# An MLP block with fewer block products: x of two row pairs transposed by the DMA engines instead of TensorE, and cast a quarter sooner

## The chip, the cores and the metric

The kernel runs on one core of a Trainium2 chip. The metric is device time in microseconds (us) of one execution. Before the change three runs took 1533.64, 1534.25 and 1534.27 us, median 1534.25.

## What is computed

```python
x:  8 x 1024 x 1024 float32     # 8192 rows of 1024
w1: 1024 x 4096 float32
w2: 4096 x 1024 float32

h = x @ w1
h = 0.5 * h * (1 + np.tanh(np.sqrt(2 / np.pi) * (h + 0.044715 * h ** 3)))
return (h @ w2).astype(np.float32)
```

## The kernel before

**Tiles.** The rows of x are taken as 64 tiles of 128 rows, numbered c, and as 32 pairs of tiles, numbered k from 0 (so the fifth and sixth pair are k = 4 and 5, with the tiles 8 to 11). The columns of w1 are taken in four ranges, numbered r. Everything is multiplied in float16: each tile of x and each range of w1 is divided by its largest value first, and the scales are put back behind the products. So a tile of x goes through a chain: `load_x` (SP issues a DMA), `look_x` (ScalarE sums the absolute values of each row), `scale_x` (VectorE, two operations on one column), `cast_x` (VectorE makes the float16 tile x16), and a transpose into `xT[k]`, whose partitions are the contracted dimension. A range of w1 goes through a similar chain: `load_w1` (eight DMAs of 512 KB; those of range 0 are issued by SP, the others by GpSimd), `look_w1` (VectorE or ScalarE), `widest_w1` (VectorE, which writes `spread`), `scale_w1` (TensorE transposes `spread` into `rows`, line 162; VectorE reduces it to the scale and its inverse), `cast_w1` and, from range 1 on, `sum_w1`.

**First product.** The first six pairs against range 0 run as plain products (class `Plain`): 28 quarters, numbered p from 0, of eight matmuls each; the four quarters 24 to 27 are pair 0 against range 1. Quarters 16 to 19 are pair 4 (tile 8 in quarters 16 and 17, tile 9 in 18 and 19), and quarters 20 to 23 are pair 5 in the same way. A quarter's sum is read by ScalarE (`e`, the tanh form of gelu, line 442), scaled to float16 by GpSimd (`g`, line 177), and the two results of a half are stored to DRAM (`gd`, line 451) by one DMA of 256 KB that SP issues. From unit 7 on (class `Quad1`) a pair and a range are multiplied as two-by-two blocks with seven block products instead of eight; these need sums of blocks of x (`sum_x`) and of w1 (`sum_w1`).

**Second product.** The stored `gd` is read back transposed, by DMA transposes, and is multiplied with sums of blocks of w2 by a scheme of 26 block products for each pair (`second`). It starts near 798 us of the span.

**Order.** All five engines follow an order that is written out by hand (`manual_schedule`). `early(p, f, ...)` puts a step behind quarter p; `between` does the same inside the first four quarters, and `plan(u, slot, ...)` inside unit u. What each engine, and the queue of DMAs that SP issues, does next is fixed by that order: an instruction that waits holds up all behind it on its engine. Each of SP's DMAs also waits for the DMA that SP issued eight before it, since there are eight completion semaphores.

**Buffers.** The pool `k2` has eleven buffers, shared in turn by `e`, `g2` (the 256 KB that a store reads), `junk` (what `look_x` writes beside its sums) and x16. A buffer is written anew only when its last reader is done: if that reader was a DMA, the next writer waits for the DMA to land.

**The lines touched.** The loop over pairs 2 to 5 (lines 637 to 649) puts `look_x` behind quarter p - 1, and `scale_x` and `cast_x` behind quarter p. p is 4 + h, 6 + h, 9 + h, 12 + h for pair 2, 3, 4, 5 and half h. The transposes of all first six pairs are `turn_x_pe` (line 209): eight TensorE transposes of 128 x 128 into a PSUM tile `turned` (line 216), and a copy into `xT` by ScalarE (line 221) for half 0 or by VectorE (line 223) for half 1. Those of tiles 8 to 11 stand behind quarters 13, 15, 17 and 19. From pair 6 on the kernel uses `turn_x` (line 203): one DMA transpose of 256 KB that SP issues (line 207).

Of the kernel before, what the change touches and what calls it, by code (L numbers as in the profile page):

```python
# [79 lines left out]
def kernel(  # L80
# [7 lines left out]
    nc = tc.nc  # L88
# [58 lines left out]
    V, S, G = nc.vector, nc.scalar, nc.gpsimd  # L147
# [477 lines left out]
    def plan(u, slot, f, *args):  # L625
        assert 0 <= u, (f, args)
        todo.setdefault((u, slot), []).append((f, args))
# [6 lines left out]
    def early(p, f, *args):  # L634
        plan(p // 4, p % 4, f, *args)

    for k in range(2, FIRST):
        for h in range(2):
            c = 2 * k + h
            p = (4, 6, 9, 12)[k - 2] + h  # L640
            early(p - 1, look_x, c)
            early(p, scale_x, c)
            early(p, cast_x, c, V)
            if h:
                early(p, factors_of_block, k, 0, V)
                early(p, factors_of_block, k, 1, G)
            if k > 3:
                early((2, 5)[k - 4], load_x, c, wpool, "w")
            early(4 * k - 2 + 2 * h - (k > 2), turn_x_pe, c, V if h else S)
    for k in first:  # L650
        for i in range(4):
            if k == 1:
# [43 lines left out]
    for k in list(middle) + list(last):  # L696
        a = at[k] if k in middle else at[last[0]]
        for h in range(2):
            c = 2 * k + h
# [206 lines left out]
```

## Time and profile before

| | |
|---|---|
| median of three runs | 1534.25 us |
| the profiled execution | 1534.61 us |
| its span | 1532.8 us |
| mean granted TensorE clock | 1.0 of full speed |
| TensorE matmul busy | 1519.6 us (99%) |
| VectorE / ScalarE / GpSimd busy | 1183.0 / 734.5 / 479.6 us |
| DMA queue that SP issues on | 71.7% of 16 engines' span |
| DMA queue that GpSimd issues on | 2.6% |

The span is the time from the first to the last instruction in the trace; 1.8 us of the execution lie outside it. PE is TensorE's matmuls, PEld its weight loads, DVE is VectorE, ACT is ScalarE, POOL is GpSimd, SP is the engine that issues most DMAs. In a list of instructions the first two columns are start and duration in us, and a bracket holds the idle time of that engine just before, with what ended it. In a list of waits the numbers are the total in us, the number of waits and the longest. In a chain of work each row is start, duration and what was running.

### The profile page before, as it was taken

To read this page: it belongs to the slowest core of one execution; us is meant where nothing else is said; L and a number is where in the kernel's file an instruction comes from. 1 tells how busy PE (TensorE), PEld (TensorE's weight loads), DVE (VectorE), ACT (ScalarE), POOL (GpSimd) and SP (SyncE) were. 2 spreads that over 40 slices of the span, in tenths; PEclk is the share of its full clock that TensorE was granted. 3 is DMA by queue.
4 is the path that set the end of the run, shared out by engine and by line. 5 is a ranking of instruction groups with operands and counts; after the bars stand their busy time and mean duration, and the time that the engine had idled before them with its cause. 6 is when DMAs were issued, how large, how long until landed. Compare 5 with 4: busy or idle time off the path is not lost.

```text
span 1532.8 us, 28623 instructions
## 1 busy us (share of the span) xinstructions
PE 1519.6 (99%) x10398; PEld 1014.1 (66%) x10398; DVE 1183.0 (77%) x2409; ACT 734.5 (48%) x1302; POOL 479.6 (31%) x592
## 2 busy tenths in 40 slices
PE   7999999999999999999999999999999999999999
PEld 4444444444444444444448888888888888888888
DVE  6897787777777777574348888888888888888886
ACT  7778777777777777787762111111111111111111
POOL 5778554556666666554440000000000000000000
PEclk9999999999999999999999999999999999999999
DMA  9754989878789787784996777766866866866872
GB/s 349 241 185 128 293 276 301 250 227 238 215 247 263 222 270 222 240 215 128 273 285 143 140 134 141 143 137 135 154 133 128 160 133 122 165 133 130 152 142 80
DMA packets 459807, 293.94 MB, mean 192 GB/s; under 512 B 333840, under 2 KB 427024, under 8 KB 459664
## 3 DMA queue, kind: packets, MB, share of 16 engines
q1 hardware_dynamic: 456208, 279.52, 71.7%
q0 software_dynamic: 3456, 12.58, 2.6%
q8 instruction: 81, 1.33, 0.4%
q14 instruction: 62, 0.51, 0.1%
HBM read 96.99 MB, written 114.29 MB: 138 GB/s over the span
## 4 chain that ended last, share of the span: by engine, by line
PE 95%; DMA 1%; POOL 1%; ACT 1%; DVE 1%; issue 0%; ACTq 0%; POOLq 0%
PE pa L402 51%; PE pc L402 30%; PE pb L402 14%; DMA gd<-g 1%; POOL g L177 1%; DMA wn<-in_w_dram 0%; ACT e L442 0%; PE pb L414 0%; POOL wn L276 0%; DMA xn<-in_x_dram 0%; ACT junk L190 0%; PE turned L216 0%; POOL w L177 0%; DVE x L179 0%; ACT xT L221 0%
## 5 line engine op out<-in xcount | busy, mean ns | idle before, releaser
L402 PEld LDWEIGHTS <-gs 128*128 128x128 f16 x4608 | 450.8, 98 | 53.0 <-DVE gs L171 0.2
L177 POOL TENSOR_SCALAR g<-e,rs 128x512 f16<-128x512 f32 x446 | 363.8, 826 | 282.6 <-ACT e L454 250.2
L402 PEld LDWEIGHTS <-xs 128*128 128x128 f16 x1936 | 189.5, 98 | 227.7
L168 DVE TENSOR_TENSOR e<-pc,e 128x512 f32<-128x512 f32 x242 | 161.5, 685 | 200.6 <-ACT e L522 199.2
L402 PEld LDWEIGHTS <-xT 128*128 128x128 f16 x1676 | 163.1, 98 | 197.0 <-issue 1.6
L402 PE MATMUL pa<-w,gs 128*128 128x256 f16 x2304 | 288.3, 273 | 0.0
L402 PE MATMUL pa<-w,xT 128*128 128x512 f16 x1080 | 255.9, 379 | 1.2 <-DVE w L179 0.5
L454 ACT ACTIVATE e<-e,us 128x512 f32<-128x512 f32 x363 | 249.0, 719 | 2.4 <-DVE e L168 2.4
L402 PE MATMUL pc<-w,xs 128*128 128x512 f16 x968 | 248.4, 379 | 0.0
L402 PE MATMUL pa<-w,xs 128*128 128x512 f16 x968 | 248.4, 379 | 0.0
L402 PEld LDWEIGHTS <-gT 128*128 128x128 f16 x2048 | 200.4, 98 | 23.2
L575 ACT ACTIVATE o<-pa,vo 128x256 f32<-128x256 f32 x96 | 45.3, 472 | 332.3 <-PE pa L402 332.3
L402 PE MATMUL pc<-w,gs 128*128 128x256 f16 x1536 | 193.8, 273 | 0.0
L402 PE MATMUL pa<-w,gT 128*128 128x256 f16 x1024 | 132.7, 273 | 0.0
L402 PE MATMUL pb<-w,xT 128*128 128x512 f16 x484 | 124.2, 379 | 0.0
L571 DVE SCALAR_TENSOR_TENSOR o<-pc,vo,o 128x256 f32<-128x256 f32 x160 | 77.0, 481 | 57.6 <-PE pc L402 57.5
L513 ACT COPY e<-pa 128x512 f32<-128x512 f32 x121 | 70.9, 586 | 92.2 <-PE pa L402 85.8
L171 DVE TENSOR_TENSOR gs<-gT,gs 128x1024 f16<-128x1024 f16 x160 | 109.7, 686 | 1.6 <-DMA gT<-gd 1.6
L571 DVE SCALAR_TENSOR_TENSOR o<-pa,vo,o 128x256 f32<-128x256 f32 x192 | 91.9, 480 | 19.3 <-PE pa L402 19.3
L402 PE MATMUL pb<-w,gs 128*128 128x256 f16 x768 | 99.5, 273 | 0.0
L402 PE MATMUL pc<-w,gT 128*128 128x256 f16 x768 | 99.5, 273 | 0.0
L503 ACT COPY e<-pa 128x512 f32<-128x512 f32 x121 | 70.0, 579 | 49.2 <-PE pa L402 49.0
(104 smaller groups left out, 1447.8 us busy)
## 6 DMA issues: line engine op xcount, KB each, us to landing
gd<-g SPq DMA_DIRECT2D x484, 128.0 KB, 3.3
wn<-in_w_dram SPq DMA_DIRECT2D x72, 512.0 KB, 5.5
xn<-in_x_dram SPq DMA_DIRECT2D x64, 512.0 KB, 5.4
out_dram<-o SPq DMA_DIRECT2D x62, 512.0 KB, 3.6
w<-wd SPq DMA_DIRECT2D x25, 512.0 KB, 5.8
wn<-in_w_dram POOLq DMA_DIRECT2D x24, 512.0 KB, 6.0
wd<-wt SPq DMA_DIRECT2D x24, 512.0 KB, 5.0
gd<-g SPq DMA_DIRECT2D x14, 256.0 KB, 5.3
```

Of the source, the lines that this page charges most:

```text
L168: V.tensor_tensor(out=o, in0=a, in1=b, op=ALU.add)
L171: V.tensor_tensor(out=o, in0=a, in1=b, op=ALU.subtract)
L177: G.tensor_scalar(out=o, in0=i, scalar1=s, scalar2=1.0, op0=ALU.mult, op1=ALU.mult)
L402: nc.tensor.matmul(bank, lhsT=left(i), rhs=right[i], start=start and i == 0, stop=i == n - 1, skip_group_check=True,)
L454: S.activation(out=e, in_=src, func=ACT.Gelu_apprx_tanh, scale=self.u[half][s])
L503: S.copy(self.e11, self.pa)
L513: S.copy(self.e12, self.pa)
L571: V.scalar_tensor_tensor(out=o, in0=ps, scalar=v, in1=o, op0=ALU.mult, op1=ALU.add)
L575: S.activation(out=o, in_=ps, func=ACT.Copy, scale=v)
```

## The change

The casts of pairs 4 and 5 move one quarter forward, with the looks ahead of them: tile 8 from quarter 9 to 8, tile 9 from 10 to 9, tile 10 from 12 to 11, tile 11 from 13 to 12 (and their looks from 8, 9, 11, 12 to 7, 8, 10, 11). `factors_of_block` of the two pairs moves with them. The TensorE transposes of tiles 8 to 11, with their copies out of PSUM, are replaced by `turn_x` on SP's queue, which stands directly behind the cast.

```diff
     for k in range(2, FIRST):
         for h in range(2):
             c = 2 * k + h
-            p = (4, 6, 9, 12)[k - 2] + h
+            p = (4, 6, 8, 11)[k - 2] + h
             early(p - 1, look_x, c)
             early(p, scale_x, c)
             early(p, cast_x, c, V)
...
             if k > 3:
                 early((2, 5)[k - 4], load_x, c, wpool, "w")
-            early(4 * k - 2 + 2 * h - (k > 2), turn_x_pe, c, V if h else S)
+            if k > 3:
+                early(p, turn_x, c, nc.sync)
+            else:
+                early(4 * k - 2 + 2 * h - (k > 2), turn_x_pe, c, V if h else S)
```

At this place SP's queue held nothing but the stores of `gd`, one for each half of a pair. Now it holds three of them as before (pair 0, and the first half of pair 1), then the transposes of tiles 8 and 9, the store of pair 1's second half, the transpose of tile 10, the store of pair 2's first half, the transpose of tile 11, the store of pair 2's second half, and the rest as before.

## The prediction

> **What bounds the kernel now.** I read the page's shares first, then the chain that ended last, then TensorE's waits.
>
> ```profile
> PE 1519.6 (99%) x10398; PEld 1014.1 (66%) x10398; DVE 1183.0 (77%) x2409; ACT 734.5 (48%) x1302; POOL 479.6 (31%) x592
> ...
> PE 95%; DMA 1%; POOL 1%; ACT 1%; DVE 1%; issue 0%; ACTq 0%; POOLq 0%
> ```
>
> TensorE is busy for all but 13.2 us and carries 95% of the chain. So work taken from it shortens the run, unless it comes back as a wait. Its waits are few:
>
> ```profile
> PE turned L216 <- ACT x L175: 7.2, 1, 7.2
> PE rows L162 <- DVE spread L155: 1.0, 1, 1.0
> ```
>
> The first is the start. The second stands at 80 us, in unit 8, after the change; no wait is listed later, so whatever TensorE has gained by then stays to the end. The chain around 80 us shows what that wait hangs on:
>
> ```profile
> 69.37 6.13 DMA wn<-in_w_dram
> 75.53 1.22 DVE w1c L150
> ...
> 79.81 0.58 DVE spread L155
> ...
> 80.43 0.33 PE rows L162
> ```
>
> A load of w1's range 2, issued by GpSimd at 69.37, lands at 75.50; VectorE then works without a gap (look, sums, spread) until 80.39. And GpSimd's list shows why that load isn't issued sooner:
>
> ```profile
> 54.71 0.70 POOL L177 TENSOR_SCALAR g<-e,rs 128x512 f16<-128x512 f32 x1
> 56.56 0.70 POOL L177 TENSOR_SCALAR g<-e,rt 128x512 f16<-128x512 f32 x1 [1.15 <-ACT e L442]
> 57.23 1.55 POOL L177 TENSOR_SCALAR w<-wn,w1i 128x1024 f16<-128x1024 f32 x1
> ...
> 68.07 1.35 POOL L177 TENSOR_SCALAR g<-e,rs 128x512 f16<-128x512 f32 x2
> 69.37 1.48 POOL L276 DMA_DIRECT2D wn<-in_w_dram  x2
> ```
>
> GpSimd waits last at 56.56, for the gelu of quarter 19; from there to 69.37 it is packed, but for about 0.5 us.
>
> **What goes.** TensorE's list around one of the removed transposes:
>
> ```profile
> 41.98 1.89 PE L402 MATMUL pc<-w,xT 128*128 128x512 f16 x8
> 43.71 0.61 PE L216 MATMUL turned<-identity,x 128*128 128x128 f16 x8
> 44.16 1.89 PE L402 MATMUL pa<-w,xT 128*128 128x512 f16 x8
> ```
>
> From the transpose's start to the next quarter's is 0.45 us (44.16 - 43.71); the other three read the same (47.61, 51.51 and 55.52 to 48.06, 51.96 and 55.97). Four make **1.80 us**. Two copies of 1.00 us go from ScalarE and two of 0.69 from VectorE; none is waited for here, so they count nothing.
>
> **What of it is kept.** Three of the four transposes stand ahead of quarter 19, so its gelu frees GpSimd 3 x 0.45 = 1.35 us sooner. GpSimd being packed from there, the load at 69.37 and the spread at 80.39 come 1.35 sooner as well. TensorE comes 1.80 sooner: the wait of 0.97 grows by 0.45, and **1.35 us** are kept.
>
> **What is moved.** Looks and casts are as many and as long as before (look 1.06 + 0.19, cast 0.75 to 1.24 us). Following ScalarE's and VectorE's order with these rows, tile 8's cast ends near 37.4 (before 38.5), tile 9's near 39.8 (39.7: a look at w1 now stands between the two), tile 10's near 44.5 (44.3), tile 11's near 45.9 (46.9). Their rows were loaded long before: SP issued them by 19.7.
>
> **What is added.** Four transposes on SP's queue, the same shape as the 52 later ones. Those landed 3.0 to 9.3 us after issue, median 5.0. TensorE needs the tiles at quarters 16, 18, 20, 22, which without the transposes start at 47.2, 50.6, 54.2 and 57.6. At 9.3 the four land at 46.7, 49.1, 53.8 and 55.2, at 5.0 by 42.4 to 50.9. So TensorE doesn't wait for them; at the bound tiles 8 and 10 are within 0.5 us of doing so. Others do wait:
>
> - ScalarE. In the order and buffers of the changed kernel, the gelu of quarter 12 writes the buffer of tile 8's x16 and so waits for that transpose, quarter 13's waits for tile 9's, quarter 16's for tile 10's, and quarter 14's for the store of pair 1's second half, which SP issued near 34.4 and which now stands behind tile 9's transpose, near 41. Without these waits quarter 12 would be read at 42.2, quarter 13 at 43.9, quarter 14 at 45.6. At 5.0 us each the waits are 0.2, 1.0 and up to 1.5 us. TensorE has three banks of each kind, so it reaches the bank of quarter 12 only at quarter 18 (50.6); covered.
> - Behind quarter 15's gelu ScalarE has the last look at w1's range 1. It began at 48.55, the spread was done at 50.78, 2.23 later, and TensorE takes it at 53.68 (52.33 after the change). So the look must begin by 50.1.
> - The DMA engines. A transpose standing alone in the stretch 147.2 to 149.2:
>
> ```profile
> DMA packets 1076, 0.29 MB, mean 146 GB/s; under 512 B 1046, under 2 KB 1076, under 8 KB 1076
> ...
> q1 hardware_dynamic: 1076, 0.29, 72.6%
> ```
>
> 72.6% of 2.0 us is 1.45 us of all sixteen engines for 256 KB. In 36 to 48 us these are at 84 to 105%, with GpSimd's loads of range 1. Two transposes (2.9 us) get ahead of the last of them, two stores of about 0.7 us fall behind: it lands 1.5 us later than the 48.3 at which it landed (issued 42.16, 6.2 us), at 49.8, against 50.1. Cover 0.3 us; I charge 0.2.
>
> The Trainium skill (Advanced Engine Details and Errata, X-Bar Transpose) says that transposing DMAs are as fast as ordinary ones, 350 to 400 GB/s. The row is 181 GB/s, so the trace doesn't agree; by the rule the last load would land near 48.3, nothing would be charged, and the sum would be -1.35.
>
> **Sum.** -1.80 + 0.45 + 0.2 = -1.15 us: the profiled execution's 1534.61 becomes 1533.46. The median of the runs is 0.36 lower, 1534.25, and becomes **1533.1**.
>
> **Rivals.**
>
> *The wait takes it all (1534.3).* The transposes get only what GpSimd's loads leave. SP's queue, and idle engines, had some 2.6 to 2.9 us of DMA time from 38.7 to 48, and two transposes need 2.9. Tile 9 then lands near 48.5, the store behind it near 50, and ScalarE's order (look, gelu of 14, of 15, look) puts the spread at 53.4: TensorE stands 1.1 us at quarter 19, and GpSimd frees itself about when it did. For it: in this stretch stores of 256 KB were slow.
>
> ```profile
> gd<-g SPq DMA_DIRECT2D x6, 256.0 KB, 5.8
> ```
>
> Against: DMA bursts between the loads, in which a store is done at once; the quickest store took 2.4.
>
> *Slower (1535.7).* The two queues take turns by packets, not bytes. A store of 256 packets lost 3.4 us (5.8 - 2.4) beside the loads; a transpose has some 1024, so it would lose four times that, 13.6, or until GpSimd's loads are through at about 47.5. Tile 8 lands at 48.3, tile 9 at 49.8, the store at 51.2; the spread is done at 55.3; GpSimd's first pair of range 2 loads goes out at 56.3 instead of 53.19. Of these 3.1 us its idle 1.15 and 0.5 take up 1.65, so the end moves by +1.45. It decides from where tile 9 lands later than 47.3, and is a loss from about 48.5. With no idle used up it would be +3.1 (1537.4). Against it: in the stretches between two loads SP's queue got most of the engines. The Trainium skill (DMA: Bandwidth & Descriptors, Queues, rings and completion order) says that each DMA engine goes round the queues packet by packet, which, with the profile's packets, is this case; no transpose stands beside GpSimd's loads in this trace.
>
> *The wait at unit 8 goes (1531.5).* GpSimd's operations in the packed stretch vary between 0.7 and 1.84 us for the same tile; if they fall well, all 1.80 and the 0.97 are gained: -2.77.
>
> *It doesn't do what it says.* The tiles come too late for TensorE itself. At 14.5 us, half as long again as the longest of the 52, tile 9 lands at 54.3, 3.7 after quarter 18 should start: 1534.25 - 1.35 + 3.7 = 1536.6.
>
> **How the numbers follow.** The forecast 0.45, the wait that takes it all 0.25, slower by turns 0.20, unit 8's wait gone 0.05, TensorE waits 0.05. 0.2% of 1534.25 is 3.1 us, about what a measurement of this kernel can tell from no change: faster than 1531.2 needs more than all the gains above (0.03); slower than 1537.3 is the far end of the turns (0.06) and TensorE's waits (0.05); within, 0.86. Range 1531.8 to 1536.6: the forecast, no gain, and the slower case's own price.
>
> **What would show it.** Right: four groups on line 216 fewer; quarter 19 starting at 52.4; the load of range 2 issued near 68.0; `rows` at 79.1 with a wait near 1.4 us; no waits of TensorE for `xT` in quarters 16 to 23. Wrong: transposes that land later than 8 us; ScalarE's gelus of 12 to 14 waiting for DMAs past 47; a wait at quarter 19; `rows` of unit 8 at 80.4 or later.

## The result, and the profile after

The changed kernel takes 1538.44 us (median of 8 runs, 1537.41 to 1540.16), against 1533.78 for the kernel before (8 runs, 1533.08 to 1534.27): a ratio of 1.0033, 95% interval 1.0023 to 1.0042. It is slower by some 4.7 us. The profiled execution of after, one of the quickest of the eight, took 1537.74 us, 3.13 more than that of before, with a span of 1536.0 (+3.2).

The page's shares differ little: TensorE still carries the chain, with 10366 matmul instructions instead of 10398 (the 32 transposes are gone) and nearly the same busy time. TensorE's waits, as the list of waits has them after the change:

```profile
PE turned L216 <- ACT x L175: 7.2, 1, 7.2
PE rows L162 <- DVE spread L155: 4.1, 1, 4.1
```

It is the same line as before the change, but another place. TensorE's lists of before and then of after show where:

```profile
51.96 1.89 PE L402 MATMUL pa<-w,xT 128*128 128x512 f16 x8
53.68 0.27 PE L162 MATMUL rows<-identity,spread 128*128 128x128 f32 x1
```

```profile
50.68 1.89 PE L402 MATMUL pa<-w,xT 128*128 128x512 f16 x8
56.64 0.45 PE L162 MATMUL rows<-identity,spread 128*128 128x128 f32 x1 [4.07 <-DVE spread L155]
56.88 3.36 PE L402 MATMUL pc<-w,xT 128*128 128x512 f16 x8
60.07 1.89 PE L402 MATMUL pa<-w,xT 128*128 128x512 f16 x8
```

Three things are to be seen. Quarter 18 starts at 50.68 instead of 51.96: the gain of three turns is there. Then TensorE stands 4.07 us for range 1's `spread`, ahead of quarter 19, where it did not wait at all before. And quarter 19 itself takes 3.19 us up to the next one's start (60.07 - 56.88) instead of 1.73. Busy times in stretches of 1 us tell why; after the five engines' busy times come the granted clock, the DMA share and GB/s:

```profile
55.00:56.00 1.00, 0.00 (x0) 0.00 (x0) 0.00 (x0) 1.00 (x3) 0.81 (x2) 1.00 1.17 357
57.00:58.00 1.00, 1.00 (x4) 0.33 (x3) 0.93 (x5) 1.00 (x3) 1.00 (x2) 0.50 0.77 259
60.00:61.00 1.00, 1.00 (x7) 0.46 (x5) 1.00 (x1) 0.67 (x1) 0.70 (x1) 1.00 0.93 210
```

The granted clock is 0.50 behind the idle time, and 1.00 again from 60 on. So the differences between the two profiled executions, at the start of each step, are these: quarter 18 -1.28; `rows` 56.64 against 53.68, +2.96; quarter 20 +4.10 (0.13 more for a slower `rows`, 1.46 for the slow quarter 19, less the fourth turn of 0.45); unit 7 +4.11; unit 8 behind its `rows` +2.92, for the wait of 0.97 that stood there is gone; the end +3.2.

What the `spread` at 56.21 hung on, by the chain of waits of after:

```profile
41.76 0.25 SPq L207
42.10 11.49 DMA gd<-g
...
54.26 0.22 ACT e L442
...
54.83 1.15 ACT junk L286 x2
...
56.21 0.30 DVE spread L155
```

A store was held at SP behind the transpose of tile 9 until 42.10 and took 11.49 us; a gelu waited for its buffer, and behind this gelu ScalarE had its last look at range 1. ScalarE's waits in 25 to 72 us (total, number, longest) show two more of the kind:

```profile
ACT e L442 <- DMA xT<-x: 7.1, 2, 4.7
...
ACT e L442 <- DMA gd<-g: 1.3, 1, 1.3
```

And the DMA view of 38 to 50 us, of before and then of after (a line of an issue: count, KB each, median us from issue to landing):

```profile
DMA packets 1530, 3.32 MB, mean 276 GB/s; under 512 B 131, under 2 KB 922, under 8 KB 1528
...
q0 software_dynamic: 686, 2.48, 60.8%
...
wn<-in_w_dram POOLq DMA_DIRECT2D x3, 512.0 KB, 6.2
```

```profile
DMA packets 2695, 2.47 MB, mean 206 GB/s; under 512 B 2174, under 2 KB 2241, under 8 KB 2693
...
q0 software_dynamic: 514, 1.85, 70.5%
...
wn<-in_w_dram POOLq DMA_DIRECT2D x3, 512.0 KB, 9.8
...
xT<-x SPq DMA_TRANSPOSE x3, 10.5
```

More was asked of the DMA engines, and less was moved: 206 GB/s instead of 276. GpSimd's queue (q0) kept them busy longer for fewer bytes: 2.48 MB in 60.8% of 12 us is 340 GB/s of busy time, 1.85 MB in 70.5% is 219. The last load of range 1, issued at 42.69, landed 10.8 us later, at 53.5; before it landed at 48.3. The four transposes landed 6.5, 10.8, 10.5 and 5.7 us after issue.

### The profile page after: what moved, and what is told of

Its sections match the earlier page's. It is cut to its first block, busy times and chain, and to the rows that moved or that the text cites. A ratio compares the mean times of both kernels' runs of the same rounds, so it can differ in the third digit from the quotient of the medians.

```text
span 1536.0 us, 28563 instructions
## 1 busy us (share of the span) xinstructions
PE 1519.5 (99%) x10366; PEld 1012.8 (66%) x10366; DVE 1177.8 (77%) x2407; ACT 731.9 (48%) x1300; POOL 477.8 (31%) x592
## 3 DMA queue, kind: packets, MB, share of 16 engines
q8 instruction: 81, 1.33, 0.4%
## 4 chain that ended last, share of the span: by engine, by line
PE 97%; DMA 1%; DVE 1%; ACT 1%; issue 0%; SPq 0%; ACTq 0%; DVEq 0%
PE pa L402 52%; PE pc L402 31%; PE pb L402 14%; DMA gd<-g 1%; DVE x L179 0%; PE pb L414 0%; DMA xn<-in_x_dram 0%; DVE w1c L150 0%; PE turned L216 0%; ACT e L442 0%; ACT junk L190 0%; ACT w L175 0%; DVE xT L223 0%; ACT x L175 0%; ACT junk L286 0%
## 5 line engine op out<-in xcount | busy, mean ns | idle before, releaser
L503 ACT COPY e<-pa 128x512 f32<-128x512 f32 x121 | 69.9, 578 | 50.1 <-PE pa L402 50.0
```

The source lines that it names most:

```text
L503: S.copy(self.e11, self.pa)
```

## Experiments

The theory formed from these two traces: a DMA transpose and GpSimd's loads, side by side in two queues, slow each other down, so that loads, transposes and the store behind them land late, ScalarE's looks with them, and TensorE stands at quarter 19; its clock then adds to it. The rivals: the moved casts; more bytes in SP's queue; more packets, as in the prediction's slower rival; the buffers that ScalarE waits for. The first four kernels ran together, then the next four, then the last four; each ran beside the kernel before, whose medians were 1533.81, 1533.70 and 1533.67.

| kernel | median us | ratio to before, 95% | wait at quarter 19, us | wait at unit 8 | loads, transposes in 38 to 50, median us to landing |
|---|---|---|---|---|---|
| before | 1533.8 | | 0 | 0.97 | 6.2, none |
| after | 1538.44 | 1.0023 to 1.0042 | 4.07 | 0 | 9.8, 10.5 |
| 1 casts alone | 1533.75 | 0.9990 to 1.0007 | 0 | 0 | 6.1, none |
| 2 transposes alone | 1541.10 | 1.0026 to 1.0054 | 4.23, at quarter 18 | 0 | 8.0, 9.8 |
| 3 loads in SP's queue | 1534.57 | 0.9996 to 1.0013 | 0.66 | 0.99 | 5.9, 5.1 |
| 4 pair 5 alone, late | 1532.91 | 0.9985 to 1.0003 | 0 | 0.20 | 5.8, 3.6 |
| 5 padded wait | 1538.87 | 1.0024 to 1.0049 | 4.53 padding + 1.20 | 1.43 | 12.1, 10.5 |
| 6 plain copies | 1533.77 | 0.9992 to 1.0010 | 0 | 0.69 | 7.6, 6.9 |
| 7 copies in small pieces | 1532.56 | 0.9987 to 1.0005 | 0 | 0 | 6.2, 6.1 |
| 8 loads on SP, pair 5 late | 1533.52 | 0.9991 to 1.0009 | 0 | 1.24 | 6.6, 4.7 |
| 9 own buffers | 1537.75 | 1.0017 to 1.0034 | 3.24 | 0 | 10.3, 8.1 |
| 10 transposes on ScalarE's queue | 1539.29 | 1.0025 to 1.0050 | 3.56 | 0 | 9.4, 10.0 |
| 11 pair 4 as changed, pair 5 late | 1539.49 | 1.0022 to 1.0050 | 4.95 | 0 | 10.4, 7.9 |
| 12 as 8, range 2 on SP too | 1532.99 | 0.9983 to 1.0001 | 0 | 0 | 6.4, 4.8 |

### 1 and 2: the two halves of the change

Casts alone, against before; TensorE's transposes stay:

```diff
-            p = (4, 6, 9, 12)[k - 2] + h
+            p = (4, 6, 8, 11)[k - 2] + h
```

> Looks and casts of pairs 4 and 5 a quarter sooner, transposes left on TensorE. Theory A (the transposes on SP's queue and GpSimd's loads of range 1 hold each other up, so the scale of range 1 is late at quarter 19): the median stays within 0.6 us of before, 1533.2 to 1534.4, and TensorE doesn't wait at quarter 19. Theory B (the new order of looks and casts on ScalarE and VectorE makes the loss): 1537 to 1540, with the wait at quarter 19.

Transposes alone, against after; the casts stand where they stood:

```diff
-            p = (4, 6, 8, 11)[k - 2] + h
+            p = (4, 6, 9, 12)[k - 2] + h
```

> Transposes of tiles 8 to 11 by DMA, issued behind the casts where these stood before (quarters 9, 10, 12, 13). Theory A: slower than before by 3 to 6 us, like the change, with a wait of 3 to 6 us at quarter 19 and transposes that take 8 to 11 us to land beside GpSimd's loads. Theory B: no loss, 1532 to 1533.

The casts cost nothing: 1533.75, and TensorE has no wait at quarter 19. The transposes alone cost it all, 1541.1. In that trace the transposes stand later and landed 6.2 to 14.1 us after issue, and one was so late that TensorE waited for the tile itself, at quarter 18 (54.81):

```profile
PE pa L402 <- DMA xT<-x: 4.2, 1, 4.2
```

### 3 and 4: the transposes without a second queue beside them

Range 1's loads issued by SP, so that they share the transposes' queue; against after:

```diff
-        (G if r else nc.sync).dma_start(
+        (G if r > 1 else nc.sync).dma_start(
```

> The change, with the eight loads of w1's range 1 issued by SP in place of GpSimd, so that loads and transposes stand in one queue, in order. If two queues are what makes them hold each other up (theory A): the transposes land in 3 to 7 us, the last load by 50, the wait at quarter 19 is under 1 us, and the median is 1532.5 to 1535. If a transpose beside loads is slow in any queue (rival): landings of 8 us and more and 1537 to 1540 again.

Pair 5 alone by DMA, behind quarters 16 and 17, when the loads have been issued; against before:

```diff
-            early(4 * k - 2 + 2 * h - (k > 2), turn_x_pe, c, V if h else S)
+            if k == 5:
+                early(16 + h, turn_x, c, nc.sync)
+            else:
+                early(4 * k - 2 + 2 * h - (k > 2), turn_x_pe, c, V if h else S)
```

> Only tiles 10 and 11 by DMA, issued behind quarters 16 and 17, when GpSimd's loads of range 1 have landed (DMA nearly idle from 49 to 53 us before); casts as before, tiles 8 and 9 on TensorE. Theory A: they land in 3 to 5 us, nobody waits for them, and two transposes of 0.45 us are saved, of which 0.45 goes into the wait at unit 8: 1532.9 to 1533.5, faster than before by 0.3 to 0.9. Rival (a DMA transpose costs wherever it stands): over 1534.5.

With all in one queue most of the loss is gone (1534.57), with the same four transposes at the same places in the order. The DMA view of 38 to 50 us of this kernel:

```profile
wn<-in_w_dram SPq DMA_DIRECT2D x4, 512.0 KB, 5.9
...
xT<-x SPq DMA_TRANSPOSE x4, 5.1
```

Of its waits, the 0.66 us at quarter 19 is the loads' place in the queue: the last was issued behind the third transpose, at 45.80 instead of 42.16. The 0.99 at unit 8 is that of before (0.97). The fourth run has its two transposes land 3.3 and 4.0 us after issue, and its median is 0.9 below that of before; the interval takes in no change.

### 5: the clock

Against after; the padding stands between quarter 18 and `rows`:

```diff
+    early(18, lambda: warm_up(w1set[0, B11][:, 0, :], 40))
     early(18, scale_w1, 1)
```

> The kernel after the change, with 40 matmuls of 256 columns put on TensorE between quarter 18 and `rows`. They read one matrix of w1 twice over into a PSUM bank that nobody reads, so they only keep TensorE busy while it waits. At full clock they take about 40 x 0.108 = 4.3 us (half of the 0.216 us that a 512-column matmul takes in the lists), about the 4.07 us that TensorE stands at quarter 19. Theory A: the granted clock of 0.50 in the stretch 57 to 59 of the profile after is the throttle's answer to those 4 us of idleness, and it alone makes quarter 19 cost 3.19 us up to the next quarter instead of 1.73. Then quarter 19 takes 1.89 us again at a clock of 1.0 in every stretch from 56 to 60; the padding overruns the wait by at most 0.5; the time is 1.0 to 1.5 us below the kernel after, at 1537.0 (1536 to 1537.6) by its median of 1538.44. Theory B: quarter 19 is slow for another reason that the padding doesn't touch (its operands or its bank come late). Then it keeps some 3.4 us and the time is 1538.4 to 1539.

```profile
52.34 4.53 PE L414 MATMUL pb<-w 128*128 128x256 f16 x40
58.07 0.30 PE L162 MATMUL rows<-identity,spread 128*128 128x128 f32 x1 [1.20 <-DVE spread L155]
58.21 1.89 PE L402 MATMUL pc<-w,xT 128*128 128x512 f16 x8
```

The mechanism is as expected: the clock was 1.00 throughout, and quarter 19 took 1.89 again. The time is not: 1538.87 instead of 1537.0. In this execution (1540.2 us) the loads landed later still (median 12.1 instead of 9.8), which was so before the padding began, and TensorE had to wait 5.73 us for the spread. So the slow clock's part, 1.46 us in the profile of after, is shown in the trace, but not found back in the medians. The eight runs of after lie 2.75 us apart (those of before 1.19), so 1.46 can be lost in how the collision's size varies; that it was lost there isn't shown.

### 6 and 7: plain copies in the transposes' places

Both against after, for tiles 8 to 11 only, in `turn_x`. Both leave out the transposition, so their products are of other numbers. Plain copies of the same 256 KB:

```diff
+            queue.dma_start(out=xT[k][:, c % 2], in_=t.rearrange("p (i n) -> p i n", n=P))
```

> The kernel after the change, but the four DMAs of tiles 8 to 11 are plain copies of x16 into the same buffers in place of transposes: the same 256 KB, the same queue, place and waits, in pieces of 2 KB (128 of them for each tile). The transposition of these four tiles is left out, so their products are of other numbers. Theory A: what hurts is how a transpose moves its data (1024 packets below 512 B for 256 KB, and the engines kept busy for it). Then the copies land within 2.4 to 5.8 us as the stores of 256 KB did, GpSimd's loads of range 1 land near 6.2 instead of 9.8, TensorE doesn't stand at quarter 19, and the time is that of the prediction, 1532.5 to 1533.8. Theory B: any further 1 MB on SP's queue in this stretch delays ScalarE's gelus and the loads. Then TensorE stands at quarter 19 for more than 2 us and the time is above 1536.

And copies in pieces of 256 B:

```diff
+            queue.dma_start(
+                out=xT[k].rearrange("p h i n -> p (h i) n")[:, c % 2::2],
+                in_=t.rearrange("p (i n) -> p i n", n=P),
+            )
```

> As the run with plain copies, but in pieces of 256 B: the eight pieces of a row of tile 8 go to every second place of the pair's buffer, those of tile 9 to the places between, and tiles 10 and 11 likewise. So each copy has 1024 pieces, about as many packets as a transpose, without transposing; the products are of other numbers again, and quarter 16 now needs tile 9 too, quarter 20 tile 11. Theory A1: the number of packets is what makes the two queues slow beside each other (the rival on record, queues that take turns by packets). Then the copies land near the 10.5 us of the transposes, the loads near 9.8, TensorE stands 3 us or more at quarter 19 or 16, and the time is 1536.5 to 1540. Theory A2: it is the transposing itself. Then the time is that of the plain copies, about 1533.

Neither loses anything. The small pieces are the sharper test, in 38 to 50 us:

```profile
DMA packets 4943, 3.74 MB, mean 312 GB/s; under 512 B 3892, under 2 KB 4391, under 8 KB 4942
...
wn<-in_w_dram POOLq DMA_DIRECT2D x3, 512.0 KB, 6.2
...
xT<-x SPq DMA_DIRECT2D x3, 256.0 KB, 6.1
```

There are more packets than in after (4943 against 2695), in the same two queues and at the same places; and there are 312 GB/s instead of 206, loads that land in 6.2 us as before, and no wait at quarter 19. So neither the bytes nor the number of packets nor the places in the order make the loss. What is left is the transposing DMA itself. Which part of it does so isn't shown: the copies differ in more than the turning, for they also held SP for 0.59 to 0.89 us an issue, where the transposes of after held it for 1.35 to 5.53.

### 8: the forecast without the collision

Range 1's loads on SP's queue as in 3, pair 5's transposes late as in 4; against 3:

```diff
-                early(p, turn_x, c, nc.sync)
+                early(p if k == 4 else 16 + h, turn_x, c, nc.sync)
```

> All four transposes by DMA and none of them beside another queue: range 1 of w1 is loaded from SP's queue (as in the third run), the transposes of tiles 8 and 9 stand where the change puts them, those of tiles 10 and 11 behind quarters 16 and 17 (as in the fourth run), behind the last load. By theory A nothing is left of the loss: the last look is done before TensorE is at quarter 19 (52.4), and all four turns of 0.45 us are saved, against a wait of some 1.0 to 1.4 us at unit 8 as in the prediction: 1532.2 to 1533.2 by the median before of 1533.8. If the transposes cost something else than the collision (theory B), the time stays at 1534.5 or above as in the third run.

The median is 1533.52, a little above the range expected. Its trace has the prediction's outline: no wait at quarter 19, all four turns saved, and a wait of 1.24 us at unit 8, for which 1.4 had been forecast; the span is 1531.6, 1.2 below that of before, where the forecast was -1.15. That the two agree so closely is luck in part. GpSimd took up the last scaling ahead of its packed stretch at 56.71, not sooner than before (56.56), and issued the load of range 2 at 69.18, where 68.0 had been forecast from 69.37; that load then landed in 4.8 us instead of 6.1. The spread now hung on ScalarE's look at the next load, which began at 77.22 after waiting 2.53 us for it. In the medians the gain is 0.2, and the interval takes in no change.

### 9: what goes through ScalarE's buffers

The float16 tiles 8 to 11 from the pool `k4`, so that no gelu waits for a transpose; against after:

```diff
-        x16[c] = k2.tile([P, H], F16, name="x16", tag="k2")
+        pool, tag = (k4, "k4") if 8 <= c < 12 else (k2, "k2")
+        x16[c] = pool.tile([P, H], F16, name="x16", tag=tag)
```

> The kernel after the change, but the float16 tiles 8 to 11 lie in the pool of the transposed tiles instead of the pool that gelu's results go through, so that no gelu writes a buffer that a transpose still reads. It tells what part of the 4.07 us at quarter 19 comes through ScalarE (gelus of quarters 12 and 13 that waited 2.4 and 4.7 us for transposes and 1.3 for a store) and what through the loads of range 1, which landed 9.8 us after issue. Theory A: the loads alone are late enough for a wait, but a smaller one. VectorE's last look at range 1 began at 51.0 for want of its load; ScalarE's last look then follows near 51 to 52 instead of 54.83, the spread is done near 53.6, TensorE waits 1 to 2 us at quarter 19 and its clock stays at 1.0: 1534.5 to 1536. Theory B: ScalarE's buffer waits count for nothing, the last load itself lands at 54: wait 3.5 us or more and 1537.4 to 1539.

The median is 1537.75, within the range of the second theory, though the wait of 3.24 us is below its 3.5. No gelu waits for a transpose now, but one still waits for the store:

```profile
53.26 0.69 ACT L443 ACTIVATE e<-pc,up 128x512 f32<-128x512 f32 x1 [3.54 <-DMA gd<-g]
```

The last load was issued at 42.53 and landed 10.5 us later, at 53.0; even a free ScalarE could not have looked at it sooner. It did look at it at 53.85, behind this gelu. So the late load accounts for some 2.4 of the 3.24 us, and the gelu's wait for the store for up to 0.85. The buffer waits on the transposes, which I had priced one by one, are not needed for most of the loss.

### 10: two hardware queues

As 3, with the transposes issued by ScalarE on its own queue; against 3:

```diff
-                early(p, turn_x, c, nc.sync)
+                early(p, turn_x, c, S)
```

> The third run (range 1 of w1 loaded from SP's queue) with the four transposes issued by ScalarE on its own queue, at the places where the change has them. So the transposes again stand beside the loads in another queue, but both queues are of the hardware kind (hardware dynamic in the profile's list), none of GpSimd's (software dynamic). Theory A: any second queue beside a transpose will do; then transposes or loads land near 10 us again and TensorE waits 2 us or more for `rows` or for `xT`: 1536 to 1540. Theory B: it takes GpSimd's queue; then both land within 3 to 7 us as in the third run, and the time is 1533.5 to 1535.5, ScalarE's four issues of 1.25 to 1.35 us each taken into account.

In 38 to 50 us (q1 is SP's queue, q10 ScalarE's):

```profile
q1 hardware_dynamic: 1450, 2.22, 61.9%
q10 hardware_dynamic: 2574, 0.64, 54.3%
...
xT<-x ACTq DMA_TRANSPOSE x3, 10.0
```

The transposes land 10.0 us after issue as beside GpSimd's queue, and the one load issued in the stretch lands after 9.4 (6.5 at most in run 3). So it doesn't take GpSimd's kind of queue. The time itself, 1539.29, proves less: ScalarE waited for its own transposes' data as well as for buffers (4.0 us for a store, 2.7 for a transpose), its looks came late for that too, and TensorE waited 1.1 us for one of its copies.

### 11: one pair is enough

Pair 4 as changed, pair 5 behind the loads; against after:

```diff
-                early(p, turn_x, c, nc.sync)
+                early(p if k == 4 else 16 + h, turn_x, c, nc.sync)
```

> Half of the change: the transposes of tiles 8 and 9 where the change puts them, beside GpSimd's loads; those of tiles 10 and 11 behind quarters 16 and 17, when the loads are through (as in the fourth run). Theory A (each transpose beside GpSimd's loads costs): tile 8 and 9 land late as before (6.5 and 10.8 us), but the loads behind them are free of tiles 10 and 11, so that the last lands sooner than in the kernel after. TensorE waits 1 to 3 us at quarter 19: 1534.5 to 1537. Theory B: the first pair's transposes alone do all the damage: 1538 or more. Theory C: it was the second pair's: 1532 to 1533.5.

```profile
PE rows L162 <- DVE spread L155: 4.9, 1, 4.9
```

Two transposes beside the loads do the whole damage (1539.49): the three loads behind them landed 10.4, 10.2 and 11.6 us after issue. I had expected a loss in proportion to the number of transposes, and it isn't; the loads that stand next to these two are late.

### 12: the best version found

As 8, with the loads of range 2 on SP's queue as well; against 8:

```diff
-        (G if r > 1 else nc.sync).dma_start(
+        (G if r > 2 else nc.sync).dma_start(
```

> The last run of the job before (all loads of range 1 on SP's queue, the transposes of tiles 10 and 11 late) with the loads of range 2 on SP's queue as well. There the wait at unit 8 was 1.24 us and hung on a load of range 2 that GpSimd issued late behind its own work. If that is right, the wait goes and the time is 1.0 to 1.3 us below that run's 1533.52: 1532.2 to 1532.6. If something else sets that spread, the wait and the time stay.

The wait of unit 8 goes, as expected. The profiles of runs 1 and 7 have no wait there either, with GpSimd issuing range 2's loads, so this one profile doesn't prove the cause. These are `rows` in the kernel of run 8, and then in this one:

```profile
78.94 0.33 PE L162 MATMUL rows<-identity,spread 128*128 128x128 f32 x1 [1.24 <-DVE spread L155]
```

```profile
78.05 0.33 PE L162 MATMUL rows<-identity,spread 128*128 128x128 f32 x1
```

1532.99 is 0.5 below run 8's median and 0.7 below before, less than the 1.0 to 1.3 expected. With run 4 (1532.91) it is the fastest here that computes the whole, but both intervals reach 1, so neither is shown to beat the kernel before.

## Why the prediction was wrong, point by point

- **What bounds the kernel, and what goes.** Right: TensorE bounds it, and three turns take 1.28 us off the start of quarter 18 (1.35 worked out).
- **What is moved.** Right: the casts ended at 37.6, 39.7, 43.9 and 45.0, and run 1 shows that they cost nothing.
- **What is kept.** The step that a gain ahead of quarter 19 makes the wait at unit 8 longer by 0.45 couldn't show in the kernel after. Where the collision is taken away (run 8) that wait is 1.24 us, 0.27 more than before. But the way there was not as worked out: GpSimd's load of range 2 was to go out 1.35 us sooner, and went out 0.19 sooner. GpSimd was not freed by the earlier gelu of quarter 19, since it was still busy with its own work. Run 12 fits a wait that hangs on the loads of range 2, but the wait at unit 8 was also 0 in runs 1 and 7 and 0.20 in run 4, where GpSimd issues these loads as before.
- **What is added: the step that failed.** "The same shape as the 52 later ones. Those landed 3.0 to 9.3 us after issue" was taken for the bound of the four new ones. But no transpose stood beside loads of another queue in the stretches from which I took that row: GpSimd issued its last load at 109.2, and the first of the 52 was issued at 146.6. Here they landed up to 10.8 us after issue (14.1 in run 2). The transpose standing alone gave 1.45 us of the engines, and from it came the last load at 49.8, as "two transposes (2.9 us) get ahead of the last of them": a sum of engine time, which holds only if work of two queues adds up. It landed at 53.5. The cover of 0.3 us at the look (50.1) was gone ten times over, and 0.2 was charged where TensorE waited 4.07 us. The slow clock behind that wait, 1.46 us, was in no term.
- **ScalarE's buffer waits.** Right in kind and order (quarters 12, 13 and 14's gelus, the store behind tile 9): 2.4, 4.7 and 1.3 us instead of 0.2, 1.0 and up to 1.5. "Covered" held for their own results; but run 9 shows that most of the loss, 4.1 us, stays when no gelu waits for a transpose.
- **The Trainium skill's rate.** Its 350 to 400 GB/s (Advanced Engine Details and Errata, X-Bar Transpose) would have put the forecast at -1.35, further from what came. The row of 181 GB/s is nearer 200: its 0.29 MB in 1.45 us hold 30 packets of a store as well. Neither rate told what a transpose does beside loads.
- **The rival "slower"** had the sequence right: tile 9 landing at 49.8 (50.6 in the trace), the store at 51.2 (53.6), the spread at 55.3 (56.5), GpSimd's first pair of range 2 loads at 56.3 (58.25), and a loss where tile 9 lands later than 48.5. Its mechanism, counted in the profile's packets, is not borne out: queues that take turns by packets would have lost as much with the small pieces of run 7, which lost nothing. That its times came out so near is then luck. Its price was short. It gave +1.45, at its far end +3.1; the profiled execution has +3.13 with 1.46 of it from the clock, which no case of the prediction held, and the medians differ by 4.7.
- **The other rivals.** "The wait takes it all" put a wait of 1.1 us at quarter 19, the right place and a quarter of the size. "The tiles come too late for TensorE itself" did not happen in the kernel after; it did in run 2. "The wait at unit 8 goes" came true, but behind a loss of 4.1 us.
- **What stays open.** Why a transpose and another queue's transfers slow each other isn't shown by any run, only that the number of packets and bytes isn't it, and that GpSimd's kind of queue isn't needed. Nor is the collision's size settled: the profiled executions of after, run 5 and run 11 had TensorE wait for its spread for 4.07, 5.73 (the padding counted as wait) and 4.95 us, in kernels whose transposes of tiles 8 and 9 stand at the same places.

## What to carry to other kernels

Before putting a DMA transpose anywhere, look at what the other queues do in those microseconds: its landing time from a stretch where it was alone, or in one queue with its neighbours, says little about a stretch where it runs beside them, and the neighbours pay too. Put it into the queue of the transfers that it would meet, or behind them: here that took the loss away (runs 3, 4 and 8), though it left no gain that the medians show. A test with plain copies in the same places tells the transposing from the traffic.

## What the runs showed of the hardware

**Transposes beside another queue.** In 38 to 50 us, 276 GB/s without transposes, 312 with plain copies in small pieces, 206 with transposes beside GpSimd's queue, 241 with transposes on ScalarE's queue beside SP's, 234 with all in one queue, where more of it was transposes (3235 packets under 512 B against 2174) and loads and transposes all landed within 6.5 us. The Trainium skill (DMA: Bandwidth & Descriptors, Rules for kernel authors) has it that a transpose next to ordinary DMAs needs nothing. It stands in a row on wrong results; for time the runs here don't agree: 4.7 us in the median.

**The clock after a wait.** Waits of 3.24, 3.56, 4.07 and 4.95 us at quarter 19 were each followed by a granted clock of 0.50, the wait of 1.20 us behind the padding was not. In the kernel after, a mean of 0.71 in 56 to 57 and of 0.58 in 59 to 60 (0.42 us and 0.16 us at full clock, the rest at half) puts the slow stretch at 56.4 to 59.8, or 3.4 us, beginning 3.8 us after quarter 18 ended (50.68 + 1.89); it cost quarter 19 1.46 us. The same working from the mean clocks of 1 us gives a slow stretch of 3.4 us in runs 9 and 10 as well (means of 0.90 at both ends in run 9, of 0.59 and 0.71 in run 10), beginning 3.4 and 3.1 us after quarter 18 ended. In run 11 it lasted 6.8 us (0.89 in 55 to 56, 0.70 in 62 to 63), and quarters 19 and 20 took 3.41 and 2.51 us up to the next instead of 1.73. The Trainium skill (TensorE: Matmul & The Clock Gate, Part 1: The HAM clock gate) says that the gate halves the clock after about 3.4 us of idleness and gives it back after as much sustained work. The trace of after agrees roughly with both: the slow stretch began 3.8 us after quarter 18 ended, and it ended 3.2 us after `rows` began. In run 11 the slow stretch was longer. In these four runs a wait of 3.24 us or more cost 1.33 to 2.46 us on top of its length; no wait between 1.20 and 3.24 us ahead of quarter 19 was measured.
